# Moving the output projection of two head groups into the filler beside the sparse mixer, and grouping value products by four blocks, in a hybrid decoder layer

## The chip, the cores and the metric

One core of one Trainium2 chip runs the whole kernel. The metric is the time of one execution on the device in microseconds (us). Times below are medians of several runs; the profile is that of one execution.

## What is computed

One layer of a decoder trunk over 1024 tokens of width 1024, in float32. Four groups of four heads (head width 64) are projected from one normalised input, each with its own attention: A differential, B forgetting, C stick-breaking, D native sparse with a compressed, a selected and a windowed branch. With 1024 tokens the selection of 16 blocks of 64 takes every block, so the selected branch is a causal attention over all keys.

```python
h = rmsnorm(x, norm_mix_g) * (1 + sc_a) + sh_a
proj = h @ w_in                                  # columns of A, B, C and D
o_a = diff_attention(...);  o_b = forgetting_attention(...)
o_c = stick_breaking_attention(...);  o_d = native_sparse_attention(...)
mixed = concatenate([o_a, o_b, o_c, o_d], -1) @ w_out
x = x + gt_a * mixed
h = rmsnorm(x, norm_ffn_g) * (1 + sc_m) + sh_m
x = x + gt_m * conv_ffn(h, w_up, conv_w, conv_b, w_down)
```

## The kernel before

The kernel is a list of operations with a planner in front of it. Each call (K.mm, K.copy, K.dma and so on) records an operation with the tiles that it reads and writes; all of them are issued from one helper, which is why every row of the profile names line 392. At the end K.schedule() plays the list through: each engine takes, of the operations that are ready, the one that was recorded first. The order of recording is thus the priority, and it also gives out the buffers: a class of tiles (line 538 and after: name, quota, group, phase) hands out its tiles strictly in the order of recording, and a class of a later phase gets only what the earlier ones of its group can't claim. PSUM has 8 banks; while the mixers run, 4 are of class S (scores), 2 of class T (all transposes), 1 of class O (values) and 1 of class pP (projections).

What is recorded in which order is written by generators. merge(main, side, per) steps through a mixer and lets a filler follow: each step of the mixer yields its weight (1.3 for each 128 keys of a step of 128 queries), times a rate from RATES, and the filler is stepped until its own yields have used that up. The mixers come in the order A, C, D, B, with the rates 0.8, 0.6, 0.3 and 1.6. Beside A, C and D the filler is side(): the input projections still missing (cq, ck, dk, dq, vb, bq, bk, each of 8 token tiles and 24 products a tile, with a normalisation and transposes after every second tile) and the compression of keys. What is left of it after D is run to its end. Then out_AC() becomes the filler of B: it loads and splits the blocks 0, 1, 4 and 5 of w_out (scaled by gt_a, split into a high and a low part), and for each of 8 token tiles loads the outputs of A and C, transposes them (class T), splits them (oT) and forms 2 x 12 products of 128x512 in pP, which VectorE adds to x (x1p) for writing to x1. The other half of the projection, for D and B, follows after B and normalises its result for the feed-forward network.

The weights of the mixers' steps: A, B and C yield 46.8 for each of two head pairs, D 85.8. A projection's token tile yields 2.56, as does half a token tile of out_AC().

pv_pair() multiplies a step's probabilities with the values. Probabilities of two 128-key blocks and two heads are transposed into one T bank, copied to a pt tile, and for each block one planned operation (mm2) does two products, whose outputs are the two halves of the partitions of O:

```python
for j in range(g0, g1):
    c = 2 * (j - g0) * 128
    K.mm2([dst[0:64], dst[64:128]], vfn(j), [pt[:, c:c + 128], pt[:, c + 128:c + 256]], j == 0, j == nb - 1)
```

Of the kernel before, what the change touches and what calls it, by code (L numbers as in the profile page):

```python
# [13 lines left out]
OP = mybir.AluOpType  # L14
# [9 lines left out]
LAM_INIT = 0.8 - 0.6 * math.exp(0.0)  # L24
TOEP = 383
CL = 126
RATES = (0.8, 0.6, 0.3, 1.6)
STEP = 1.3
EARLY = 2
DCUT = (2, 3, 3, 3)  # L30

CA_Q, CA_K, CA_V = 0, 256, 512
CB_Q, CB_K, CB_V, CB_F = 768, 1024, 1280, 1536
# [110 lines left out]
class Program:  # L144
# [274 lines left out]
    def mm2(self, outs, lhsTs, rhss, start, stop):  # L419
# [6 lines left out]
        d = max(d, 1.26 * self._mm_use(lhsTs[0], rhss[0]))  # L426
        self.op([("PE", d, f)], list(lhsTs) + list(rhss), list(outs)).share = 2.0 * self._mm_use(lhsTs[0], rhss[0]) / d

    def tr(self, out, in_, ident):
        self.op([("PE", 109.0, self._call("tensor", "transpose", (out, in_, ident), {}))], [in_, ident], [out])  # L430

# [69 lines left out]
def layer_kernel(ctx: ExitStack, tc, x, c, rel_bias, ada_w, ada_b, norm_mix_g, norm_ffn_g, w_in, w_out,  # L501
# [4 lines left out]
    K = Program(tc)  # L506
    NB, NH = 33, 28
    pool = lambda n, b, **k: ctx.enter_context(tc.tile_pool(name=n, bufs=b, **k))
    cp, bp, hp, sp = pool("cp", 1), pool("bp", 1), pool("hp", 1), pool("sp", 1)
# [7 lines left out]
    def const(shape, dt=F32, name="const"):  # L517
        ncls[0] += 1
        k = f"c{ncls[0]}_{name}"
        K.klass(k, 1, "c", 0)  # L520
        return K.tile(k, shape, dt, name)

    def dram(shape, name):
        ncls[0] += 1
        k = f"d{ncls[0]}_{name}"
        K.klass(k, 1, "d", 0)
        return K.tile(k, shape, F32, name)
# [6 lines left out]
    for name, quota, group, phase in (  # L534

# [7 lines left out]

# [6 lines left out]

# [2 lines left out]
        K.klass(name, quota, group, phase)  # L553

    def blk(cls, dt=F32, shape=(128, 1024)):
        return K.tile(cls, shape, dt)

    def hb(cls, dt=F32):
        return K.tile(cls, (128, 512), dt)

    def ps1(cls):
        return K.tile(cls, (128, 512))


    ident = const([128, 128], name="ident")
# [55 lines left out]
    def halves(h):  # L621
        return slice(h * 512, h * 512 + 512)
# [42 lines left out]
    def row_tile(cls, src):  # L665
        t = blk(cls)
        K.dma(t, src.strided(0, [[0, 128], [1, D]]), 524288)
        return t
# [76 lines left out]
    def split_w(hcls, raw, shape):  # L745
        hi, lo = blk(hcls, F32R, shape), blk(hcls, F32R, shape)
        K.copy(hi, raw, ("ACT",))
        K.tt(lo, raw, hi, OP.subtract, ("POOL",))
        return hi, lo
# [70 lines left out]
    def qk_proj(name, col, scale, norm=None, early=False):  # L820
        return proj([(col, 256)], 256, qk_post([split_out((name, p), scale) for p in range(2)], norm and (norm, 0)), early=early)
# [68 lines left out]
    def pv_pair(P, n, vfn, dst):  # L890

        nb = n // 128
        for g0 in range(0, nb, 2):
            g1 = min(nb, g0 + 2)
            t = ps1("T")
            for j in range(g0, g1):
                for u in range(2):
                    c = 2 * (j - g0) + u
                    K.tr(t[:, c * 128:(c + 1) * 128], P[u][:, j * 128:(j + 1) * 128], ident)
            pt = hb("pt")  # L900
            w = (g1 - g0) * 256
            K.copy(pt[:, :w], t[:, :w])
            for j in range(g0, g1):
                c = 2 * (j - g0) * 128
                K.mm2([dst[0:64], dst[64:128]], vfn(j), [pt[:, c:c + 128], pt[:, c + 128:c + 256]], j == 0, j == nb - 1)

    def back(o):

# [121 lines left out]
    def compress():  # L1030
        kv = blk("kv")
        kvs.append(kv)

        def keep(jj, ps):
            K.copy(kv[:, jj * 256:jj * 256 + 256], ps)
        yield from proj([(CD_KC, 128), (CD_KS, 64), (CD_KW, 64)], 256,
                        qk_post([keep, split_out(("dk", 0), g_sw)], (64, 128)))
# [229 lines left out]
    def merge(main, side, per):  # L1267

        acc = 0.0
        for t in main:  # L1270
            acc += per * t
            while acc > 0.0:
                d = next(side, None)
                if d is None:
                    break
                acc -= d

    def chain(*gs):
        for g in gs:
            yield from g  # L1280

    def run_all(g):
        for _ in g:
            pass

    def heads(stacks, attn):
        for p in range(2):
            yield from attn(p, stacks(p))
# [68 lines left out]
    gta_row, gtm_row, ada_m = dram([1, D], "gta_row"), dram([1, D], "gtm_row"), {}  # L1357
# [15 lines left out]
    done = set()  # L1373

    def side():

        gs = [("cq", qk_proj("cq", CC_Q, 0.125)), ("ck", qk_proj("ck", CC_K, 1.0)), ("dk", compress()),
              ("dq", qk_proj("dq", CD_Q, g_dq, 64)), ("cmp", compress_kv()), ("vb", proj([(CB_V, 256)], 256, post_vb)),
              ("bq", qk_proj("bq", CB_Q, g_bq, 64)), ("bk", qk_proj("bk", CB_K, g_bk, 64))]
        next(gs[0][1])  # L1380
        for a, (name, g) in enumerate(gs):
            if a + 1 < len(gs):
                next(gs[a + 1][1])
            yield from g
            done.add(name)

    fill = side()
    for need, g, rate in (("", heads(stacks_A, attn_A), RATES[0]), ("ck", heads(stacks_C, attn_C), RATES[1]),
                          ("cmp", heads(stacks_D, attn_D), RATES[2])):
        while need and need not in done:  # L1390
            next(fill)
        merge(g, fill, rate)
    run_all(fill)


    gt_a = row_tile("gta", gta_row)
    wo_hi, wo_lo = {}, {}

    def load_wo(ks):
        for k in ks:  # L1400
            raw = blk("wor")
            K.dma(raw, w_out[0, k * 128:(k + 1) * 128, :], 524288)
            K.tt(raw, raw, gt_a, OP.mult, ("POOL",))
            wo_hi[k], wo_lo[k] = split_w("wo", raw, (128, 1024))

    def o_part(i, c0, c1, pcls):
# [14 lines left out]
    def o_mul(ps, hl, ks, n):  # L1421
        m = 0
        for t, k in enumerate(ks):
            for a, b in ((hl[0], wo_hi), (hl[1], wo_hi), (hl[0], wo_lo)):
                K.mm(ps, a[:, t, :], b[k][:, halves(n)], m == 0, m == 11)
                m += 1

    x1 = {}

    def out_AC():  # L1430
        load_wo((0, 1, 4, 5))
        yield 0
        for i in range(NT):
            hl = o_part(i, (0, 2), (4, 6), "T")
            x1[i] = dram([128, 1024], f"d_x1_{i}")
            for n in range(2):
                ps = ps1("pP")
                o_mul(ps, hl, (0, 1, 4, 5), n)
                xt = hb("x1p")
                K.dma(xt, x[0, i * 128:(i + 1) * 128, halves(n)], 262144)  # L1440
                K.tt(xt, ps, xt, OP.add)
                K.dma(x1[i][:, halves(n)], xt, 262144)
                yield 2.56
        load_wo((6, 7, 2, 3))
    oac = out_AC()
    next(oac)
    merge(heads(stacks_B, attn_B), oac, RATES[3])
    run_all(oac)

# [152 lines left out]
    chain, kept_b = {}, {}  # L1602
# [55 lines left out]
    def down_mul(n, ps=None):  # L1658
# [3 lines left out]
        q0 = 0  # L1662
        for c in DCUT:
            ops = {}
# [58 lines left out]
    done = K.schedule()  # L1723
# [29 lines left out]
```

## Time and profile before

| | us |
|---|---|
| median of 3 runs | 1491.72 |
| all three | 1491.72, 1485.66, 1492.05 |
| the profiled execution | 1490.82 |
| its span, first to last instruction | 1489.1 |

The mean granted clock of TensorE over the profiled span is 0.978 of full speed. In the profile PE is TensorE's products, PEld its loads of the stationary operand, DVE is VectorE, ACT ScalarE, POOL GpSimd and SP the queue of most DMAs. The stages follow each other by their tiles: A until about 376 us, C until 514, D until 677, B until 786, then the second half of the output projection with the normalisation, and from about 875 us the feed-forward network.

### The profile page before, as it was taken

Reading aid. Unit: us, or ns where it says so; the run is one execution under the profiler, and the core shown is the slowest. Engines: PE = TensorE matmul, PEld = TensorE weight load, DVE = VectorE, ACT = ScalarE, POOL = GpSimd, SP = SyncE. Lnnn points to the kernel's source line nnn. Section 1 sums busy time; section 2 is a strip of 40 time slices with the busy share of each in tenths; the row PEclk is TensorE's granted clock in tenths of the full one; section 3 lists DMA queues with packets and bytes.
Section 4 is the critical chain, followed back from the end, with each engine's and each line's share of the span. In section 5 each row is a group of like instructions: output and inputs, shape, how many; then the busy total and the mean of one; then the engine's idle time right before and its main releaser. Section 6 shows DMA issues by size and latency. Waiting matters only on the chain.

```text
span 1489.1 us, 24140 instructions
## 1 busy us (share of the span) xinstructions
PE 1389.8 (93%) x8573; PEld 1174.1 (79%) x8573; DVE 1120.2 (75%) x2382; ACT 703.0 (47%) x1529; POOL 217.3 (15%) x249
## 2 busy tenths in 40 slices
PE   3999999999799998999999789999999999999998
PEld 2878888888687886777877568888888888888886
DVE  7966668999779986775475886666666665898777
ACT  2531245657678655663364644334444443453342
POOL 3543310223323355100000000000000000000000
PEclk9999999999899998999999899999999999999999
DMA  9679463535431423145534322222222224963675
GB/s 353 209 213 319 134 171 93 170 91 155 114 76 49 133 92 98 41 105 162 161 105 155 113 86 86 80 83 85 85 85 80 84 85 169 370 238 99 226 248 170
DMA packets 169963, 211.24 MB, mean 142 GB/s; under 512 B 25517, under 2 KB 112214, under 8 KB 169842
## 3 DMA queue, kind: packets, MB, share of 16 engines
q1 hardware_dynamic: 168338, 208.52, 44.9%
q0 software_dynamic: 1504, 1.17, 0.5%
q8 instruction: 67, 1.10, 0.3%
q14 instruction: 54, 0.44, 0.1%
HBM read 165.30 MB, written 47.89 MB: 143 GB/s over the span
## 4 chain that ended last, share of the span: by engine, by line
PE 71%; DVE 12%; ACT 2%; issue 1%; DMA 1%; POOL 0%; SPq 0%; DVEq 0%; POOLq 0%; ACTq 0%
PE up L392 28%; PE dn L392 14%; PE pP L392 10%; PE T L392 7%; PE O L392 5%; PE S L392 4%; DVE P L392 4%; PE op L392 3%; ACT P L392 1%; DVE S L392 1%; DVE m L392 1%; DVE pt L392 1%; DVE nt L392 1%; DVE gB L392 1%; DVE hl L392 1%
## 5 line engine op out<-in xcount | busy, mean ns | idle before, releaser
L392 PE MATMUL up<-gB,fw 128*128 128x512 f32 x1320 | 303.6, 389 | 5.7 <-DVE fw L392 2.9
L392 PEld LDWEIGHTS up<-gB,fw 128*128 128x128 f32 x1320 | 247.5, 188 | 58.2 <-DVE fw L392 3.3
L392 PE MATMUL dn<-ds 128*128 128x512 f32 x924 | 209.9, 389 | 0.2 <-DVE ds L392 0.2
L392 PEld LDWEIGHTS dn<-ds 128*128 128x128 f32 x924 | 173.4, 188 | 36.6 <-DVE ds L392 0.6
L392 PE MATMUL pP<-wh,hT 128*128 128x256 f32 x1344 | 198.3, 292 | 3.4 <-DVE nt L392 1.3
L392 PEld LDWEIGHTS pP<-wh,hT 128*128 128x128 f32 x1344 | 178.7, 195 | 9.3 <-DVE nt L392 2.1
L392 ACT ACTIVATE P<-S,nm 128x512 f32<-128x512 f32 (+3 forms) x240 | 135.4, 571 | 81.9 <-DVE nm L392 63.6
L392 PE MATMUL S<-kst,qst 128*128 128x512 f32 (+2 forms) x480 | 134.0, 372 | 9.7 <-ACT P L392 5.7
L392 PE MATMUL up<-gA,fw 128*128 128x512 f32 x528 | 126.8, 395 | 7.6 <-DVE fw L392 7.6
L392 PE MATMUL T<-ident,P 128*128 128x128 f32 x696 | 113.1, 285 | 14.9 <-ACT P L392 8.9
L392 PEld LDWEIGHTS up<-gA,fw 128*128 128x128 f32 x528 | 99.8, 190 | 29.2 <-DVE fw L392 8.6
L392 PEld LDWEIGHTS T<-ident,P 128*128 128x128 f32 x696 | 79.8, 144 | 33.6 <-issue 15.1
L392 PEld LDWEIGHTS S<-kst,qst 128*128 128x128 f32 x480 | 79.1, 193 | 22.8 <-ACT P L392 9.0
L392 ACT COPY pt<-T 128x512 f32<-128x512 f32 (+1 forms) x106 | 56.5, 539 | 67.3 <-PE T L392 66.2
L392 DVE COPY pt<-T 128x512 f32<-128x512 f32 (+1 forms) x94 | 58.5, 627 | 38.6 <-PE T L392 36.1
L392 DVE TENSOR_REDUCE m<-S 128x1 f32<-128x512 f32 (+3 forms) x160 | 76.6, 488 | 7.5 <-PE S L392 6.7
L392 ACT CAST ds<-dg 128x512 fp32r<-128x512 f32 x82 | 48.2, 619 | 63.7 <-DVE dg L392 40.3
L392 DVE TENSOR_TENSOR fw<-fr,fw 128x512 fp32r<-128x512 f32 x110 | 75.1, 684 | 0.0
L392 ACT CAST fw<-fr 128x512 fp32r<-128x512 f32 x110 | 67.5, 614 | 9.6 <-DVE fw L392 9.5
L392 ACT ACTIVATE P<-P 128x256 f32<-128x256 f32 (+8 forms) x98 | 64.9, 690 | 11.5 <-POOL P L392 7.5
L392 PE MATMUL O<-pt,V 128*64 128x128 f32 x864 | 65.7, 287 | 4.2 <-DVE pt L392 2.3
L392 DVE SCALAR_TENSOR_TENSOR acc<-ada,cact,acc 128x512 f32<-128x512 f32 (+1 forms) x70 | 66.5, 950 | 3.1 <-DMA ada<-in_ada_w_dram 1.9
(295 smaller groups left out, 2323.2 us busy)
## 6 DMA issues: line engine op xcount, KB each, us to landing
dg<-d_g SPq DMA_DIRECT2D x99, 256.0 KB
fr<-in_ffn_w_up_dram SPq DMA_DIRECT2D x88, 256.0 KB
ada<-in_ada_w_dram SPq DMA_DIRECT2D x64, 256.0 KB
dg<-in_ffn_w_down_dram SPq DMA_DIRECT2D x55, 256.0 KB
d_g<-va SPq DMA_DIRECT2D x22, 512.0 KB
ada<-in_ada_w_dram SPq DMA_DIRECT2D x16, 512.0 KB
wr<-in_w_in_dram SPq DMA_DIRECT2D x32, 256.0 KB
x<-in_x_dram SPq DMA_DIRECT2D x8, 512.0 KB
```

Of the source, the lines that this page charges most:

```text
L392: return getattr(getattr(self.nc, eng), meth)(*a, **k)
```

## The change

The rate beside D goes from 0.3 to 0.45. out_AC() is no longer the filler of B alone: it is chained behind side(), so that one filler runs through all four mixers, and what follows the projection bk in it is the loading of the output weights and the projection of A and C. The row gt_a is loaded inside out_AC() and no longer between D and B. B stays at 1.6 for whatever filler is left. In pv_pair() the products of up to four blocks (PVB) are recorded as one operation, mms, behind the transposes and copies of all of them, and class pt has 4 tiles instead of 3. The planner costs such a group at 190 ns and 1.03 times the time of its pairs.

```diff
-RATES = (0.8, 0.6, 0.3, 1.6)
+RATES = (0.8, 0.6, 0.45, 1.6)
+PVB = 4
...
+    def mms(self, prods):
+        fs = [self._call("tensor", "matmul", (o, a, b), dict(start=st, stop=sp)) for o, a, b, st, sp in prods]
+        def f():
+            return [g() for g in fs][-1]
+        d = len(prods) * 0.5 * 1.03 * self._mm_use(prods[0][1], prods[0][2]) + 190.0
+        u = len(prods) * self._mm_use(prods[0][1], prods[0][2])
+        self.op([("PE", d, f)], [x for p in prods for x in p[1:3]], [p[0] for p in prods]).share = u / d
...
-            ... ("pt", 3, "h", 2), ...
+            ... ("pt", 4, "h", 2), ...
...
-        for g0 in range(0, nb, 2):
-            g1 = min(nb, g0 + 2)
-            t = ps1("T")
...
-                K.mm2([dst[0:64], dst[64:128]], vfn(j), [pt[:, c:c + 128], pt[:, c + 128:c + 256]], j == 0, j == nb - 1)
+        for h0 in range(0, nb, PVB):
+            h1 = min(nb, h0 + PVB)
+            pts = []
+            for g0 in range(h0, h1, 2):
+                g1 = min(h1, g0 + 2)
+                t = ps1("T")
...
+                pts += [pt[:, c:c + 128] for c in range(0, w, 128)]
+            K.mms([(dst[64 * u:64 * u + 64], vfn(j)[u], pts[2 * (j - h0) + u], j == 0, j == nb - 1)
+                   for j in range(h0, h1) for u in range(2)])
...
-    fill = side()
-    for need, g, rate in (("", heads(stacks_A, attn_A), RATES[0]), ("ck", heads(stacks_C, attn_C), RATES[1]),
-                          ("cmp", heads(stacks_D, attn_D), RATES[2])):
-        while need and need not in done:
-            next(fill)
-        merge(g, fill, rate)
-    run_all(fill)
-    gt_a = row_tile("gta", gta_row)
...
     def out_AC():
+        gt_a.append(row_tile("gta", gta_row))
         load_wo((0, 1, 4, 5))
         yield 0
...
-    oac = out_AC()
-    next(oac)
-    merge(heads(stacks_B, attn_B), oac, RATES[3])
-    run_all(oac)
+    fill = chain(side(), out_AC())
+    for need, g, rate in (("", heads(stacks_A, attn_A), RATES[0]), ("ck", heads(stacks_C, attn_C), RATES[1]),
+                          ("cmp", heads(stacks_D, attn_D), RATES[2]), ("", heads(stacks_B, attn_B), RATES[3])):
+        while need and need not in done:
+            next(fill)
+        merge(g, fill, rate)
+    run_all(fill)
```

## Rows read from the trace of the kernel before

**Rows 1.** The page: the span, the busy time of the engines (us, share of the span, instructions), and one line of the span in 40 equal slices (busy tenths of TensorE).
```profile
span 1489.1 us, 24140 instructions
...
PE 1389.8 (93%) x8573; PEld 1174.1 (79%) x8573; DVE 1120.2 (75%) x2382; ACT 703.0 (47%) x1529; POOL 217.3 (15%) x249
...
PE   3999999999799998999999789999999999999998
```

**Rows 2.** The table of stages: a stretch in us from the span's start, its length, then busy us and (instructions) of PE, PEld, DVE, ACT and POOL, then the granted clock of TensorE, the DMA engines' busy share and GB/s.
```profile
514.00:534.00 20.00, 18.73 (x161) 16.20 (x160) 17.30 (x48) 10.29 (x28) 9.60 (x6) 1.00 0.54 172
534.00:573.00 39.00, 39.00 (x358) 33.00 (x357) 27.88 (x70) 21.85 (x55) 24.32 (x26) 1.00 0.28 82
573.00:591.00 18.00, 11.18 (x59) 8.60 (x59) 17.17 (x61) 10.22 (x32) 8.05 (x5) 0.73 0.12 41
591.00:634.00 43.00, 39.58 (x340) 32.26 (x337) 30.71 (x101) 25.93 (x77) 9.37 (x5) 0.95 0.25 65
634.00:677.00 43.00, 39.62 (x368) 32.54 (x367) 31.75 (x119) 25.54 (x75) 2.93 (x3) 0.96 0.36 91
677.00:743.00 66.00, 66.00 (x392) 52.42 (x392) 30.65 (x66) 19.05 (x50) 0.68 (x1) 1.00 0.56 178
743.00:786.00 43.00, 42.00 (x381) 33.25 (x377) 31.09 (x91) 23.94 (x67) 0.00 (x0) 1.00 0.33 97
```

**Rows 3.** The same view in slices of 20 us, in the second half of the sparse mixer; the columns are those of Rows 2.
```profile
590.00:610.00 20.00, 18.02 (x165) 14.88 (x161) 12.91 (x47) 11.04 (x31) 7.82 (x4) 0.96 0.53 140
610.00:630.00 20.00, 18.56 (x154) 14.80 (x152) 14.71 (x51) 13.26 (x40) 1.59 (x2) 0.91 0.05 14
630.00:650.00 20.00, 17.20 (x145) 14.39 (x144) 14.05 (x44) 10.47 (x27) 1.04 (x1) 0.91 0.35 93
```

**Rows 4.** The tiles of the output projection: instructions with count, duration in ns (smallest/median/largest), first and last start in us, form.
```profile
L392 PE MATMUL T<-ident,oin x32: 270/272/332, 675.8 to 733.9; 128*128 128x128 f32 x32
...
L392 ACT CAST oT<-T x8: 585/586/586, 676.5 to 734.2; 128x512 fp32r<-128x512 f32 x8
L392 DVE TENSOR_TENSOR oT<-T,oT x8: 680/680/692, 677.5 to 735.0; 128x512 fp32r<-128x512 f32 x8
...
L392 DVE TENSOR_TENSOR x1p<-pP,x1p x16: 691/692/693, 681.3 to 742.4; 128x512 f32<-128x512 f32 x16
```

**Rows 5.** The timeline, two instructions: a start in us, its duration in us, engine, line, operation. The write of C's last results, and the end of the split of the fourth of eight blocks of output weights.
```profile
515.46 0.45 SPq L392 DMA_DIRECT2D o_dram<-on  x1
...
545.45 2.36 POOL L392 TENSOR_TENSOR wo<-wor,wo 128x1024 fp32r<-128x1024 f32 x1 [3.26 <-ACT wo L392]
```

**Rows 6.** The timeline of TensorE: a run of twelve products of the output projection and what follows it.
```profile
682.29 2.89 PE L392 MATMUL pP<-wo,oT 128*128 128x512 f32 x12
685.11 0.66 PE L392 MATMUL O<-pt,V 128*64 128x128 f32 x8
```

**Rows 7.** The timeline of TensorE: runs of value products (128x64, written to O) and the instruction after each; 214.88 is the first and 782.07 the last of 74 runs on V, 523.51 the first and 672.30 the last of 46 runs on VD.
```profile
214.88 0.44 PE L392 MATMUL O<-pt,V 128*64 128x128 f32 x4 [0.42 <-DVE pt L392]
...
523.51 0.44 PE L392 MATMUL O<-pt,VD 128*64 128x128 f32 x4
...
534.80 0.44 PE L392 MATMUL O<-pt,VD 128*64 128x128 f32 x4
535.17 0.66 PE L392 MATMUL T<-ident,P 128*128 128x128 f32 x4
...
557.43 1.09 PE L392 MATMUL T<-ident,P 128*128 128x128 f32 x8
558.28 0.94 PE L392 MATMUL S<-kst,qst 128*128 128x512 f32 x3
...
559.15 1.09 PE L392 MATMUL O<-pt,VD 128*64 128x128 f32 x16
560.18 0.66 PE L392 MATMUL T<-ident,P 128*128 128x128 f32 x4
...
672.30 1.31 PE L392 MATMUL O<-pt,VD 128*64 128x128 f32 x20
...
782.07 1.09 PE L392 MATMUL O<-pt,V 128*64 128x128 f32 x16
```

**Rows 8.** The timeline of VectorE: the results of B that are scaled for writing, first head pair's second half, then the second pair's first.
```profile
754.63 0.68 DVE L392 TENSOR_TENSOR on<-T,rlb 128x512 f32<-128x512 f32 x1
...
763.30 0.68 DVE L392 TENSOR_TENSOR on<-T,rlb 128x512 f32<-128x512 f32 x1
```

**Rows 9.** The page's groups for the copies of transposed probabilities (busy us, mean ns of one | idle before), and from the tile view of O the idle time ahead of value products by what ended it (us, times).
```profile
L392 ACT COPY pt<-T 128x512 f32<-128x512 f32 (+1 forms) x106 | 56.5, 539 | 67.3 <-PE T L392 66.2
L392 DVE COPY pt<-T 128x512 f32<-128x512 f32 (+1 forms) x94 | 58.5, 627 | 38.6 <-PE T L392 36.1
...
  ACT pt L392: 8.8, 19
...
  DVE pt L392: 6.8, 17
```

**Rows 10.** The timeline around the end of the filler: the last products of bk, the last step of their normalisation on VectorE, and the transposes that end the wait (in brackets the engine's idle time before and what ended it).
```profile
572.58 0.62 PE L392 MATMUL pP<-wh,hT 128*128 128x256 f32 x3
...
583.53 2.70 DVE L392 TENSOR_TENSOR nt<-nt,qk_y 128x256 f32<-128x256 f32 x2
585.95 1.24 PE L392 MATMUL T<-ident,nt 128*128 128x128 f32 x4 [3.53 <-DVE nt L392]
```

More of the change, by code (lines that the diff above doesn't have):

```diff
@@ L892, in pv_pair @@
         nb = n // 128
-        for g0 in range(0, nb, 2):
-            g1 = min(nb, g0 + 2)
-            t = ps1("T")
[L896 to L904, printed above, removed]
-                K.mm2([dst[0:64], dst[64:128]], vfn(j), [pt[:, c:c + 128], pt[:, c + 128:c + 256]], j == 0, j == nb - 1)
+        for h0 in range(0, nb, PVB):
[4 more added lines that the diff above has]
+                t = ps1("T")
+                for j in range(g0, g1):
+                    for u in range(2):
+                        c = 2 * (j - g0) + u
+                        K.tr(t[:, c * 128:(c + 1) * 128], P[u][:, j * 128:(j + 1) * 128], ident)
+                pt = hb("pt")
+                w = (g1 - g0) * 256
+                K.copy(pt[:, :w], t[:, :w])
+                pts += [pt[:, c:c + 128] for c in range(0, w, 128)]
+            K.mms([(dst[64 * u:64 * u + 64], vfn(j)[u], pts[2 * (j - h0) + u], j == 0, j == nb - 1)
+                   for j in range(h0, h1) for u in range(2)])
     def back(o):
@@ L1385, in side @@
             done.add(name)
-    fill = side()
-    for need, g, rate in (("", heads(stacks_A, attn_A), RATES[0]), ("ck", heads(stacks_C, attn_C), RATES[1]),
-                          ("cmp", heads(stacks_D, attn_D), RATES[2])):
-        while need and need not in done:
-            next(fill)
-        merge(g, fill, rate)
-    run_all(fill)
-    gt_a = row_tile("gta", gta_row)
-    wo_hi, wo_lo = {}, {}
+    wo_hi, wo_lo, gt_a = {}, {}, []
     def load_wo(ks):
@@ L1402, in load_wo @@
             K.dma(raw, w_out[0, k * 128:(k + 1) * 128, :], 524288)
-            K.tt(raw, raw, gt_a, OP.mult, ("POOL",))
+            K.tt(raw, raw, gt_a[0], OP.mult, ("POOL",))
             wo_hi[k], wo_lo[k] = split_w("wo", raw, (128, 1024))
```

2 rows, old and new, of the table k are left out of this document.

## The prediction

> **What bounds the kernel now.** I read the page's shares first, then the table of stages, then 20 us slices of the lossy one, then single instructions. TensorE is busy for 93% of the span; VectorE for 75%, ScalarE 47%, and no other engine comes near [rows 1]. A busy TensorE gains nothing from a new order, so the question is only where it is idle or runs at the lower of its two clock levels (1.2 instead of 2.4 GHz). The feed-forward network, from 875 us on, is solid. Before it the table of stages shows a pattern [rows 2]. While the sparse mixer D has filler beside it, TensorE works 39.00 of 39 us (534 to 573). Then the filler ends: 11.18 of 18 us at a mean clock of 0.73, and after that 39.58 and 39.62 of 43 us at 0.95 and 0.96. From 677 on the output projection of A and C lies beside B: 66.00 of 66 us at 1.00. B's rest, 743 to 786, has no filler either, yet loses only 1.00 of 43 us. So the change moves filler from B, which hardly needs it, to the part of D that does.
>
> **Where the moved work can start.** The projection's transposes take banks of class T, and each class hands out its tiles in the order of the program text. Before, these tiles stood behind all of D's, so the first one runs at 675.8 us [rows 4], although the four blocks of weights that it needs were split at 545.45 + 2.36 = 547.8 us, and C's last results went out at 515.46 [rows 5]; neither weights nor data are an obstacle. The loading of the weights itself (GpSimd, ScalarE, SP queue) ran beside D already; buffers set its pace, and its place in the order gains nothing. Now the tiles stand inside D. Filler is dealt out by credits: side() holds 150.9 of them, A and C draw 0.8 x 93.6 + 0.6 x 93.6 = 131, and D's own steps sum to 171.6. At 0.3 the remaining 19.9 last for 66 of D's 171.6 units (the filler's end at 573 us); at 0.45 they last for 44, and the projection's 16 x 2.56 = 41 go until unit 135. That covers the stretch that lost most and leaves D's last 36 units and all of B without.
>
> **Part 1, D's lossy stretch is filled.** Loss by slices of 20 us, from 590 to 650 [rows 3]: idle 1.98 + 1.44 + 2.80 = 6.2 us. Time at the lower level is twice (1 - clock) x 20: 1.6 + 3.6 + 3.6 = 8.8 us; TensorE was busy in 53.8 of the 60 us and does half the work at that level, so 8.8 x 0.90 / 2 = 4.0 us. Together 10.2 us. A filled stretch isn't free of loss: 514 to 573 left 1.27 us of 59 idle [rows 2], so some 118 us (this stretch and the moved work) lose 2.5, and 7.7 are left; as D's last 36 units stay bare, I take **-7 us**; bounds -10.2 (filled as 534 to 573) and -1 (the idle time stays, rival 1).
>
> **Part 2, B opens without filler.** The moved work is 16 x 12 products and 32 transposes. A run of 12 products begins at 682.29 and the next instruction at 685.11 us [rows 6], so 0.235 us each and 45 in all; eight transposes take 557.43 to 558.28 us [rows 7], 0.11 each, 3 in all. In the 66 us from 677 on B therefore got 18 us of work done, and this is the part that now has no cover. At the loss of 743 to 786 (1.00 of 43) it costs 0.4 us; at that of D's 610 to 650, idle 4.2 and slow 3.2 of 40 us [rows 3], 3.3 us. The first is the nearer: same mixer, and it holds the change from one head pair to the next (results at 754.63 and 763.30 [rows 8]). I take **+1.5**. B's end isn't bare: the last projection starts to fill in as soon as the first token tiles of the second pair are out.
>
> **Part 3, value products in fours.** Where a run of value products (128x64) starts and where the next instruction starts gives its price: 1 block 534.80 to 535.17, 0.37 us, 4 blocks 559.15 to 560.18, 1.03 us [rows 7] (four records of the trace are one block). That is 0.22 a block and 0.15 a run. The text had 196 groups of two blocks and now has 120 of four (24 for each of A, B, C, 48 for D). But in the trace the twos already stand together: 120 runs, 74 on V and 46 on VD [rows 7] (the first and the last of each stand there). What can still join are the 24 groups whose remainder is one or two blocks: its copy ends during the 1.03 us of the full four. 24 x 0.15 = 3.6, of which TensorE gains what it is bound for, some nine tenths: **-3**, bounds 0 and -7. The other side is that eight products now wait for the later of two copies (0.54 on ScalarE, 0.63 on VectorE [rows 9]). Idle ahead of value products on a copy was 8.8 + 6.8 = 15.6 us for 120 runs [rows 9], 0.13 each; if it doubles where no filler is (some 36 groups) that is +4.7. Behind a waiting group stand, in TensorE's order, the next transposes and scores, and for them both copying engines; the list of ready work can put them first, so **+1**, bounds 0 and 4.7. The fourth pt buffer takes a place that has no other taker in D and B; nothing. In A and C the order changes by part 3 alone.
>
> A row for a rule: the 0.15 us a run is what a change between 128x128 and 128x64 tiles costs here. The Trainium skill, TensorEngine Tiling (Array Packing), section Key Properties, says that a change of tiling mode drains the engine; the trace agrees. Taken by itself, from groups as the text has them, it would give 76 changes fewer, 76 x 0.15 = 11 us; the count of runs above says that they were already gone.
>
> **Part 4, the stall at the filler's end.** bk's last products end at 573.2 us; their normalisation goes through a chain of VectorE, ScalarE and GpSimd steps that ends from 583.53 on, and their transposes come at 585.95, after 3.53 us of idle TensorE, with all of D's later T tiles behind them [rows 10]. The 18 us lose 6.82 idle and 9.7 slow x 0.62 / 2 = 3.0 [rows 2]. The same last step exists after the change, earlier in D, and what follows it needs a T bank as well. I leave it at **0**: bounds -7 (denser filler brings the last step before D needs its turn) and +4 (the next T tiles wait for two DMAs of o_dram that can only be issued then). DMAs of the moved step, 2 + 4 for each token tile, pass the SP queue in D, where the DMA engines are used 0.25 to 0.36 [rows 2]; POOL issues nothing new. VectorE gets 0.68 + 2 x 0.69 = 2.1 us for each of 8 tiles [rows 4], against 62.5 of 86 us used from 591 to 677 [rows 2]: it has room.
>
> **Sum.** -7 + 1.5 - 3 + 1 + 0 = -7.5 us. The profiled execution took 1490.82 us (span 1489.1 and 1.7 around it), so **1483 us**. It lies 0.9 us under the median of the three runs, 1491.72, whose lowest is 1485.66; against the median it is -0.6%. About 0.5% (7.5 us, so a bound at 1484.3) is what a measurement of this kernel can tell from no change.
>
> **Rivals.** (1) The gain does not come: D's idle time is not a lack of work but the order of T tiles, as at 585.95, and the moved work queues in the same order. Part 1 is then -1, the time 1489. For it: in the stall of [rows 10] no filler could go ahead. Against: 534 to 573, 39.00 of 39 us in the same mixer with filler.
> (2) B alone is as lossy as D's 610 to 650: part 2 is 3.3 and, as D's bare end loses likewise, part 1 is 1 less: the sum -4.7, 1486. Against it 743 to 786.
> (3) Slower: a T bank as the bound. Each token tile holds one of the two T banks from its transpose (675.8) over ScalarE's cast (676.5) to the end of VectorE's subtraction (677.5 + 0.7) [rows 4], 2.4 us, in a stage whose every block needs those banks. If D's transposes stand still for all of it, 8 x 2.4 = 19 us come on top: 1502. It decides from 1.9 us a tile on, (7.5 + 7.5) / 8. Against: B shared the banks in the same way and TensorE was busy 66.00 of 66 us; but D's VectorE is fuller.
> (4) The stall of part 4 is covered: -7 more, 1476.
> (5) The fours join as strongly as the twos did, 196 to 120: then 120 become 73, -7 instead of -3: 1479. The rule of the Trainium skill's page above carries no further than this.
>
> **How the numbers follow.** Forecast (1478 to 1488) 0.40, rival 1 0.20, rival 2 0.10, rival 3 0.10, rival 4 0.12, rival 5 0.08. Two thirds of the forecast's own spread lie under 1484.3, so faster is 0.26 + 0.12 + 0.08 = 0.46; slower (above 1499) is rival 3 with a little of the bounds' far ends, 0.11; same 0.43. The range takes in rivals 1, 2, 4 and 5 with some of their spread and leaves rival 3 out: 1473 to 1496.
>
> **What would show it.** Transposes from oin beginning near 560 us and not at 676; the projection's products spread over some 100 us of D; TensorE near 100% at clock 1.00 there; D ending near 720 us; B from there to 779 at 95% or more; runs of value products below 105 in number; a T tile that waits 10 us or more near 555 to 570 (part 4). Wrong would be: idle slices in D beside unfinished projection work (rivals 1 and 3), clock under 0.95 in B (rival 2), or a feed-forward stage that takes another length than before, which nothing here touches.

## The result, and the profile after

The changed kernel takes 1472.57 us (median of 4, 1470.88 to 1473.88) against 1491.88 us before (median of 4): ratio 0.9885, 95% interval 0.9861 to 0.9909. It is faster, as forecast, but by 1.15% and not by 0.6%, and it lies 0.4 us under the low end of the range. The profiled execution took 1470.88 us.

The page's first lines of the changed kernel (span; busy us, share and instructions of each engine), which answer to [rows 1]:

```profile
span 1469.2 us, 24142 instructions
...
PE 1379.6 (94%) x8573; PEld 1171.3 (80%) x8573; DVE 1118.4 (76%) x2384; ACT 701.1 (48%) x1524; POOL 226.7 (15%) x252
```

The span is 19.9 us shorter, the busy time of TensorE 10.2 us. The table of stages, with the columns of [rows 2], until the filler's end, the stall, D beside the projection, D's end, B:

```profile
513.00:550.00 37.00, 35.49 (x314) 32.11 (x314) 28.89 (x79) 21.41 (x56) 26.13 (x21) 1.00 0.48 148
550.00:565.00 15.00, 11.73 (x101) 9.90 (x100) 13.79 (x32) 6.96 (x21) 9.09 (x13) 0.94 0.18 42
565.00:673.00 108.00, 107.76 (x784) 88.72 (x783) 66.83 (x204) 50.35 (x135) 16.87 (x8) 0.99 0.42 135
673.00:706.00 33.00, 31.41 (x301) 25.83 (x301) 28.61 (x112) 21.46 (x66) 2.55 (x2) 1.00 0.41 95
706.00:765.00 59.00, 58.09 (x531) 47.32 (x528) 42.39 (x125) 37.20 (x107) 0.00 (x0) 1.00 0.35 96
```

D is now full where it was lossy: beside the projection TensorE works 107.76 of 108 us. The stall at bk's end is 15 us with 11.73 busy, where it was 18 with 11.18. B, now without the projection of A and C beside it, loses 0.91 of 59 us. The projection's transposes run in D, from 558.3 and not from 675.8 us [rows 4]:

```profile
L393 PE MATMUL T<-ident,oin x32: 270/273/332, 558.3 to 664.0; 128*128 128x128 f32 x32
```

Value products, TensorE's timeline: the first and the last run on VD, a long run and what follows it, the last run on V. Over the whole trace there are 98 runs, 63 on V and 35 on VD. Counted in the same way the kernel before has 119; [rows 7] and the prediction have 120, because one run on VD that lay across the edge of two windows of the timeline was counted twice:

```profile
520.42 0.44 PE L393 MATMUL O<-pt,VD 128*64 128x128 f32 x4
...
577.20 1.97 PE L393 MATMUL O<-pt,VD 128*64 128x128 f32 x32
579.10 0.66 PE L393 MATMUL T<-ident,oin 128*128 128x128 f32 x4
...
699.76 1.31 PE L393 MATMUL O<-pt,VD 128*64 128x128 f32 x20
...
760.93 1.09 PE L393 MATMUL O<-pt,V 128*64 128x128 f32 x16
```

Eight blocks in one run take 1.90 us (577.20 to 579.10), which is 8 x 0.22 and one 0.15, as in [rows 7].

**Where the time went.** C's last result is issued for writing at 515.46 us before [rows 5] and at 512.80 now, B's last at 785.73 and 764.57. So the 19.9 us are 2.7 before D, 18.5 in D and B (270.3 to 251.8 us), and -1.2 behind B. For the same stretch I add up, in slices of 10 us, the idle time of TensorE and half of its busy time at the lower clock level: 15.9 + 6.2 = 22.1 us before, 7.5 + 1.7 = 9.2 now. The rest of the stretch, 248.2 and 242.6 us, is work at full clock. So 12.9 us are lost time that is gone and 5.6 us are less work. The forecast had 5.5 for the first (parts 1, 2, 4) and 2 for the second (part 3).

### The profile page after: what moved, and what is told of

It reads as the page before. It is cut to its first block, busy times and chain, and to the rows that moved or that the text cites. A ratio compares the mean times of both kernels' runs of the same rounds, so it can differ in the third digit from the quotient of the medians.

```text
span 1469.2 us, 24142 instructions
## 1 busy us (share of the span) xinstructions
PE 1379.6 (94%) x8573; PEld 1171.3 (80%) x8573; DVE 1118.4 (76%) x2384; ACT 701.1 (48%) x1524; POOL 226.7 (15%) x252
## 4 chain that ended last, share of the span: by engine, by line
PE 71%; DVE 13%; issue 2%; ACT 2%; POOL 1%; DMA 0%; POOLq 0%; DVEq 0%; ACTq 0%
PE up L393 28%; PE dn L393 14%; PE pP L393 10%; PE T L393 7%; DVE P L393 4%; PE S L393 4%; PE O L393 4%; PE op L393 3%; DVE pt L393 1%; DVE m L393 1%; DVE S L393 1%; ACT P L393 1%; DVE gB L393 1%; DVE nt L393 1%; DVE hl L393 0%
## 5 line engine op out<-in xcount | busy, mean ns | idle before, releaser
L393 ACT ACTIVATE P<-P 128x128 f32<-128x128 f32 (+8 forms) x98 | 64.0, 690 | 20.1 <-POOL P L393 16.3
L393 DVE SCALAR_TENSOR_TENSOR cv<-ga,ccol,cv 128x1023 f32<-128x1023 f32 (+1 forms) x44 | 56.5, 1283 | 15.8 <-ACT cv L393 15.0
```

What stands on the lines that cost most here:

```text
L393: return getattr(getattr(self.nc, eng), meth)(*a, **k)
```

## The experiments

The table has all runs. Loss and work are those of D and B, worked out as above from each run's profiled execution; the ratio is against the kernel before in the same rounds. Held is explained in part 3: in the same stretch, what VectorE's instructions beside GpSimd's operations on output weights took beyond their usual time (the median of their kind beside no instruction of GpSimd), counted where it is over 0.2 us.

| kernel | us | ratio, 95% | runs of value products | D and B, us | loss | work | held, us |
|---|---|---|---|---|---|---|---|
| before | 1491.88 | | 119 | 270.3 | 22.1 | 248.2 | 8.6 |
| changed | 1472.57 | 0.9885 (0.9861 to 0.9909) | 98 | 251.8 | 9.2 | 242.6 | 6.7 |
| fours alone | 1478.41 | 0.9928 (0.9909 to 0.9946) | 99 | 259.5 | 16.7 | 242.8 | 6.1 |
| move alone | 1493.66 | 1.0031 (1.0011 to 1.0051) | 121 | 270.7 | 21.0 | 249.7 | 16.5 |
| changed, pairs in mms | 1476.02 | 0.9924 (0.9898 to 0.9950) | 116 | 255.0 | 7.8 | 247.2 | 4.2 |
| changed, rate 0.3 | 1485.44 | 0.9972 (0.9955 to 0.9989) | 98 | 266.2 | 22.3 | 243.9 | 3.8 |
| before, pairs in mms | 1489.85 | 1.0000 (0.9982 to 1.0019) | 115 | 262.7 | 16.4 | 246.3 | 10.3 |
| changed, old price | 1475.35 | 0.9904 (0.9871 to 0.9937) | 97 | 247.2 | 5.2 | 242.0 | 4.3 |
| changed, weights on VectorE | 1471.74 | 0.9867 (0.9833 to 0.9900) | 99 | 253.1 | 9.0 | 244.1 | 0 |
| move alone, weights on VectorE | 1478.66 | 0.9913 (0.9886 to 0.9939) | 120 | 255.2 | 7.2 | 248.0 | 0 |
| before, weights on VectorE | 1481.49 | 0.9939 (0.9920 to 0.9959) | 117 | 262.5 | 15.0 | 247.5 | 0 |
| fours alone, weights on VectorE | 1475.63 | 0.9901 (0.9881 to 0.9920) | 100 | 255.7 | 11.1 | 244.6 | 0 |
| changed, price 150 | 1476.20 | 0.9902 (0.9881 to 0.9924) | 97 | 256.8 | 13.6 | 243.2 | 11.1 |
| before, price 1.30 | 1487.49 | 0.9987 (0.9970 to 1.0003) | 116 | 261.9 | 15.1 | 246.8 | 6.3 |

D and B are not the whole difference. C's last write goes out between 510.9 and 524.4 us, and latest in three kernels whose planner has another price for value products: 520.0 in changed with pairs in mms, 518.1 in before with pairs in mms, 524.4 with the old price. What these save in D and B they partly lose in A and C, and a profiled execution can lie some us off its kernel's median.

**1. The parts one by one.** Fours alone is the kernel before with the new pv_pair, mms and the fourth pt tile; move alone is the changed kernel with the old pv_pair:

```diff
 # fours alone, against the kernel before
-            K.mm2([dst[0:64], dst[64:128]], vfn(j), ...)
+            K.mms([... for j in range(h0, h1) for u in range(2)])
-  ("pt", 3, "h", 2)
+  ("pt", 4, "h", 2)
 # move alone, against the changed kernel: the same lines turned round
```

> The kernel before with the value products in fours (mms, PVB 4, four pt tiles) and nothing else: filler, rates and place of the output projection as before. Theory M (the move carries the gain: TensorE's idle time and low clock in D vanish, the fours only save some 20 runs of 0.15 us): 3 to 6 us faster than before, about 1487, the losses between 573 and 650 us stay. Theory K (the fours carry it, by fewer runs and by a planner whose price for a run is nearer to the chip): 10 us or more, 1481 or less.

> The changed kernel with value products in twos as before (mm2, three pt tiles): only the filler is chained and the rate beside D is 0.45. Theory M: 13 to 15 us faster than before, 1477 to 1479, with about 120 runs of value products and D nearly without idle time beside the projection. Theory K: at most the forecast's 7 us, 1484 or more.

Both expectations of theory M fell, and both times lie in theory K's ranges. The fours alone gave 0.72%, the move alone nothing: it is 0.1 to 0.5% slower. In the fours alone two stretches of stages, the 18 us behind bk's end and D's bare stretch, read:

```profile
562.00:580.00 18.00, 17.71 (x183) 15.03 (x181) 16.79 (x64) 13.05 (x39) 8.17 (x11) 1.00 0.41 108
580.00:665.00 85.00, 76.77 (x669) 64.42 (x666) 63.39 (x219) 52.61 (x153) 17.63 (x10) 0.92 0.28 77
```

The loss of the bare stretch is still there (76.77 of 85 us, clock 0.92), but the stall is not: 17.71 of 18 us, where [rows 2] had 11.18 at a clock of 0.73. Nothing in the fours makes a stall of bk's normalisation shorter. And in the move alone D beside the projection isn't full; its rows for that stretch and for B:

```profile
569.00:690.00 121.00, 113.10 (x789) 90.75 (x790) 73.22 (x211) 49.53 (x135) 17.25 (x8) 0.97 0.38 120
723.00:784.00 61.00, 59.36 (x529) 45.74 (x530) 42.40 (x128) 38.66 (x108) 0.00 (x0) 1.00 0.35 93
```

7.90 of 121 us are idle there, at a clock of 0.97, although the same products as in the changed kernel are its filler. So the filler was in the right place and something else held TensorE up.

**2. Price and rate.** The planner charges the new groups otherwise than the old ones, and it settles the order. Pairs in mms is the changed kernel, and in a second run the kernel before, with the new operation for two blocks; old price charges the fours 269 ns a block; and the rate alone was put back:

```diff
-PVB = 4
+PVB = 2
 # the changed kernel; the same with the projection beside B
...
-        d = len(prods) * 0.5 * 1.03 * self._mm_use(...) + 190.0
+        d = len(prods) * 0.5 * max(self._mm_time(...), 1.26 * self._mm_use(...))
...
-RATES = (0.8, 0.6, 0.45, 1.6)
+RATES = (0.8, 0.6, 0.3, 1.6)
```

> The changed kernel with PVB 2: the new operation and its price (190 ns a run) stay, the groups are of two blocks again. If the fours matter by what is joined, the runs rise towards 120 and the time by 3 us or so, to 1475 to 1477, like the move alone. If they matter by the planner's truer price, the time stays at 1471 to 1474.

> The kernel before with the new operation and its price of 190 ns a run, but groups of two blocks (PVB 2), four pt tiles, the output projection beside B as before. Theory R (the planner's price of a run makes the better order): about as fast as the fours alone, 1476 to 1481. Theory J (what is joined counts): 118 to 120 runs and the time of before, 1487 to 1491. Theory N (every order of the planner is a draw, since it does not know which small VectorE operations will stand behind a GpSimd operation): anything from 1476 to 1493.

> The changed kernel with its groups of four, but the planner charges them as it charged the twos, 269 ns a block and nothing for the run. Theory R: the gain of the price goes, 1482 or more. Theory J: 100 runs or so and 1471 to 1475. Theory N: between, and the loss sits where small VectorE operations run beside GpSimd.

> The changed kernel with the old rate 0.3 beside D: the projection of A and C still follows side() in the filler, but begins at unit 66 of D's 171.6 and some 9 of its 41 credits are left for B. If the gain is that D's bare stretch is filled, nearly all of it stays, 1473 to 1478, with the stall at bk's end back near 573 us at its old size of about 10 us. If the rate matters by itself, 1480 or more.

The price isn't it (theory R): pairs at the new price gain nothing beside B (1.0000), and fours at the old price keep nearly all, 0.9904 and 97 runs. These two, and the changed kernel with pairs, came within 0.4 us of theory J's ranges, but the move alone is no 1475 to 1477. What the column of work shows is the grouping: seven kernels with pairs need 246.3 to 249.7 us, 247.7 on average, seven with fours 242.0 to 244.6, 243.3 on average. That is 4.4 us, in every order. The loss has no such rule: 5.2 to 22.3 us. The move alone and changed with pairs, both with groups of two and the projection in D, lie at 21.0 and 7.8, and 17.6 us apart in time. They differ in the price, in two blocks being one operation, and in the fourth pt tile; no run tells these three apart. That fits theory N, whose range nearly any time would have fitted.

The old rate was a miss: I expected 1473 to 1478, it is 1485. Its stretch beside the projection, the change from D to B, and TensorE's first scores of B:

```profile
571.00:704.00 133.00, 123.74 (x915) 100.58 (x915) 82.24 (x265) 61.45 (x177) 17.46 (x10) 0.96 0.40 121
704.00:725.00 21.00, 19.95 (x120) 15.61 (x119) 12.30 (x33) 7.73 (x22) 0.00 (x0) 0.84 0.19 64
...
703.74 1.29 PE L393 MATMUL S<-kst,qst 128*128 128x512 f32 x4 [3.38 <-DMA qst<-d_bq]
```

Spread over 150 us the projection no longer fills D (9.26 of 133 us idle, clock 0.96), and at the start of B the scores wait 3.38 us for their DMA, which nothing covers. So the rate belongs to the gain, as far as one order can show it.

**3. Who holds TensorE up.** In the move alone, 588 us, one line each for GpSimd, VectorE (two), ScalarE and TensorE:

```profile
588.00 2.36 POOL L393 TENSOR_TENSOR wor<-wor,gta 128x1024 f32<-128x1024 f32 x1 [3.73 <-DMA wor<-in_w_out_dram]
...
588.11 2.27 DVE L393 TENSOR_TENSOR dl<-dl 128x8 f32<-128x8 f32 x1
590.30 0.35 DVE L393 CUSTOM_DVE_ANT_0 S<-S,bias,nm 128x128 f32<-128x128 f32 x1
...
590.74 0.69 ACT L393 ACTIVATE P<-S,nm 128x512 f32<-128x512 f32 x1 [3.23 <-DVE nm L393]
...
591.92 0.55 PE L393 MATMUL T<-ident,oin 128*128 128x128 f32 x3 [1.40 <-ACT P L393]
```

GpSimd scales a block of output weights, 2.36 us from 588.00. VectorE begins an addition of 8 columns at 588.11 and needs 2.27 us for it: it ends when GpSimd does. The minima queued behind it come 2 us late, ScalarE's exponentials after 3.23 us of waiting, and TensorE, whose order is fixed, stands 1.40 us in front of a transpose of the filler's own (oin), with the filler's products behind it. The stall of [rows 10] has the same in it. Two operations of VectorE there, one free and one beside GpSimd, and GpSimd's two:

```profile
580.72 0.16 DVE L392 TENSOR_TENSOR qk_t<-qk_t,qk_y 128x8 f32<-128x8 f32 x1
581.34 2.00 DVE L392 TENSOR_TENSOR qk_y<-qk_y,qk_t 128x8 f32<-128x8 f32 x1
...
580.97 2.35 POOL L392 TENSOR_TENSOR wo<-wor,wo 128x1024 fp32r<-128x1024 f32 x1 [3.52 <-ACT wo L392]
583.28 2.34 POOL L392 TENSOR_TENSOR wor<-wor,gta 128x1024 f32<-128x1024 f32 x1
```

An operation of 8 columns takes 0.16 us, the next 2.00; the scaling in [rows 10] that starts at 583.53 takes 2.70 beside the second GpSimd operation and, in a kernel without these, 0.76. In the changed kernel one such wait is left in the stall, 3.30 us:

```profile
546.61 3.03 PE L393 MATMUL pP<-wh,hT 128*128 128x256 f32 x24
...
557.68 3.30 DVE L393 TENSOR_TENSOR qk_t<-ss,qk_y 128x8 f32<-128x8 f32 x1
561.01 0.17 DVE L393 TENSOR_TENSOR qk_t<-qk_t,qk_y 128x8 f32<-128x8 f32 x1
...
558.59 2.35 POOL L393 TENSOR_TENSOR wo<-wor,wo 128x1024 fp32r<-128x1024 f32 x1
...
562.19 0.30 PE L393 MATMUL T<-ident,nt 128*128 128x128 f32 x1 [3.27 <-DVE nt L393]
```

The Trainium skill, SBUF — State Buffer, section Who interferes with whom, says so: VectorE's second SBUF port pair is GpSimd's, and a VectorE instruction with two inputs in SBUF contends with a GpSimd instruction that reads there. The traces agree, and give the price: the small operation ends with GpSimd's, in these lines 1.8 to 3.1 us late. The planner knows nothing of it, so which small operation meets which block of weights is a draw.

The column held adds such waits up. In D and B of all 14 traces no VectorE instruction went more than 0.2 us over its usual time without an instruction of GpSimd beside it. The move alone has the most, 10 instructions and 16.5 us. Among the five kernels with the projection in D at rate 0.45 and the weights on GpSimd, the loss goes with it, but for the first two, which are nearly equal: 4.2, 4.3, 6.7, 11.1 and 16.5 us held, 7.8, 5.2, 9.2, 13.6 and 21.0 us lost. That is also what sets the move alone apart from changed with pairs, whose order avoids most of the waits with GpSimd's work in place. It isn't all of the loss: at the old rate 22.3 us are lost with 3.8 held.

To test it, all 16 operations on output weights go to VectorE, in all four combinations of the two parts:

```diff
-            K.tt(raw, raw, gt_a[0], OP.mult, ("POOL",))
-            wo_hi[k], wo_lo[k] = split_w("wo", raw, (128, 1024))
+            K.tt(raw, raw, gt_a[0], OP.mult, ("DVE",))
+            wo_hi[k], wo_lo[k] = blk("wo", F32R), blk("wo", F32R)
+            K.copy(wo_hi[k], raw, ("ACT",))
+            K.tt(wo_lo[k], raw, wo_hi[k], OP.subtract, ("DVE",))
```

> The move alone, value products in twos as before, with the scaling and the low part of the output weights on VectorE. Theory P: it is these waits that ate the gain of the move alone (1493.7): now 1478 to 1486, and the filled stretch of D has under 3 us of idle TensorE in place of 7.9. Rival (the twos as such keep D from being filled): 1490 or more.

> The changed kernel with the scaling and the low part of the output weights on VectorE instead of GpSimd: 16 operations of 128x1024, about 1.1 us each, 18 us more on VectorE and 38 less on GpSimd. Theory P (in D small VectorE operations stand behind GpSimd's weight operations, and the exponentials and TensorE behind them): 2 to 6 us faster than the changed kernel, 1466 to 1470, no operation of 8 columns over 0.3 us in D, the stall at bk's end shorter by 3 us. Rival: VectorE's extra work costs as much as it saves, 1472 to 1478.

> The kernel before with the scaling and the low part of the output weights on VectorE; nothing else. Theory P (waits of small VectorE operations behind GpSimd's weight operations cost time wherever a plan lets them meet): the stall at bk's end loses the 3.5 us that two such waits added to it, and D some more: 1480 to 1486. Rival Q (those waits hurt only where the filler is moved into D): 1488 to 1492, the extra 18 us of VectorE bring nothing.

> The fours alone with the weight operations on VectorE: with the run before and the earlier ones this fills a table of four (twos or fours, projection beside B or in D) without GpSimd in the way. If the gain of the fours alone (11.5 us) was their own, it is 11 us here as well, measured against the kernel before with the weights on VectorE. If it came from an order that happened to avoid those waits, it is 3 to 5 us here, 1476 to 1481, what 20 fewer runs of 0.15 us give.

The move alone falls from 1493.7 to 1478.7 us, the kernel before from 1489.4 in those rounds to 1481.5, the fours alone from 1478.4 to 1475.6, and the changed kernel stays (1472.6 and 1471.7). The first two lie in theory P's ranges; the changed kernel's 1471.7 lies between P's range and the rival's. The fours alone gain 0.38%, 6 us, over the kernel before with its weights on VectorE, and not their 11.5, so by these medians a part of them came from the order; 1475.6 is 0.4 us below the range expected for that. The planner's order changes with the edit as well, so these times alone don't prove the waits; but in the move alone the loss falls from 21.0 to 7.2 us as the 16.5 us held go. The stall is nearly gone in the kernel before without GpSimd's operations, while its bare stretch is as lossy as ever:

```profile
559.00:577.00 18.00, 16.63 (x160) 13.16 (x159) 15.21 (x52) 11.86 (x30) 6.51 (x10) 1.00 0.44 128
577.00:668.00 91.00, 82.85 (x727) 68.65 (x726) 70.11 (x244) 54.27 (x164) 5.76 (x5) 0.94 0.26 68
```

In the changed kernel the chain behind bk now has its normal durations, and TensorE waits 0.78 us in place of 3.27:

```profile
554.04 0.16 DVE L393 TENSOR_TENSOR qk_t<-ss,qk_y 128x8 f32<-128x8 f32 x1
556.26 0.16 DVE L393 TENSOR_TENSOR qk_y<-qk_y,qk_t 128x8 f32<-128x8 f32 x1
556.74 0.76 DVE L393 TENSOR_TENSOR nt<-nt,qk_y 128x256 f32<-128x256 f32 x2
...
557.31 0.30 PE L393 MATMUL T<-ident,nt 128*128 128x128 f32 x1 [0.78 <-DVE nt L393]
```

Yet the filled stretch isn't free of idle time. In the move alone with the weights on VectorE:

```profile
564.00:680.00 116.00, 112.03 (x812) 90.60 (x811) 75.20 (x214) 49.90 (x135) 5.14 (x6) 1.00 0.39 125
```

3.97 of 116 us, where I expected under 3. And in the changed kernel with the weights on VectorE:

```profile
557.00:675.00 118.00, 113.43 (x819) 92.89 (x819) 73.93 (x215) 52.36 (x143) 2.56 (x2) 0.99 0.37 117
```

4.57 of 118 us idle, with nothing held. So the changed kernel's 0.24 of 108 was a good draw of the order, and what it gains in the stall without GpSimd's operations it loses here.

**4. How much is a draw.** Two prices of the planner were moved a little; no instruction is added or left out:

```diff
 # the changed kernel
-        d = ... + 190.0
+        d = ... + 150.0
 # the kernel before, in mm2
-        d = max(d, 1.26 * self._mm_use(lhsTs[0], rhss[0]))
+        d = max(d, 1.30 * self._mm_use(lhsTs[0], rhss[0]))
```

> The changed kernel with the planner's price of a run at 150 ns in place of 190; no instruction is added or left out, only the order moves. It measures how much a time depends on the draw of an order. If little: 1471 to 1475. If the order is a draw with the GpSimd waits as its dice: up to 1483.

> The kernel before with its price for value products at 1.30 instead of 1.26, 9 ns more a block; no instruction is added or left out. If the order matters little: 1487 to 1492. If the kernel before was a bad draw: 1480 to 1486, and a stall at bk's end that is shorter than 10 us.

3.6 us more for the one, 1 us above what I expected if the order matters little; 1.9 less for the other, inside that range, though its stall is shorter (2.5 us of TensorE idle from bk's last product to the end of its transposes, for 6.7 in the kernel before). Neither interval is clear of the kernel it started from. So single differences of 2 to 4 us between these kernels prove nothing, and the 17.6 us of part 2 show that an order can be worth far more. What stands is the averages of seven and the waits that were read in the traces.

## Why it came out so

| | pairs | fours |
|---|---|---|
| projection beside B, weights on GpSimd | 1 | 0.9928 |
| projection in D, weights on GpSimd | 1.0031 | 0.9885 |
| projection beside B, weights on VectorE | 0.9939 | 0.9901 |
| projection in D, weights on VectorE | 0.9913 | 0.9867 |

Below, where GpSimd is out of the way, the parts add up: the move gives 0.26% and 0.34% (4 and 5 us), the fours 0.38% and 0.46% (6 and 7 us), both 0.72%, 10.7 us. Only the sum is well clear of the intervals; the two differences of the move are not. Above they don't add up: -0.31 and 0.43% for the move, 0.72 and 1.46% for the fours. The difference between above and below is what GpSimd's operations on the weights cost: 0.61% or 9 us in the kernel before, 0.18% or 3 us in the changed one. So of the 17 us some 11 are the change's own, and some 6 come because the new order happens to suffer less from GpSimd. That is luck, and how it comes about isn't shown: the time held itself only falls from 8.6 to 6.7 us. Each of these differences holds a draw of the order too, so the shares are rough. The 15 us that the move alone gets back go with 16.5 us held that are gone.

**Parts 1 and 2, -7 and +1.5: about right, with luck.** By the tables of stages, D behind the stall loses 10.4 us before and 2.9 after, B 1.0 before (677 to 786) and 0.9 after: -7.5 and 0. But the move alone did not bring that, and the filled stretch of the changed kernel was a good draw. Once nothing of GpSimd's disturbs it, the move by itself gives 4 to 5 us for a forecast of 5.5, within the noise of these runs. Where it starts (558 us for a forecast of 560), what it covers and how little B loses without it (0.91 of 59 us) came as forecast; D ended at 706 and not at 720 us because of the other parts.

**Part 3, -3 and +1: mis-sized.** The fours give 6 to 7 us. 21 runs fewer came, for 24 forecast, and a run costs 0.15 us. But the work in D and B falls by 4.4 us, while the 16 runs that D and B have fewer (70 to 54) account for 2.4. Summed up by tiles, from one product's start to the next at full clock, the value products give 2.2 us of the 4.4; 0.9 are products of the input projections, of which 4 to 5 more run before C's last write and so are no saving; most of the rest is in scores and transposes, and its cause is open. The +1 for waiting on the second copy doesn't show: idle time ahead of value products on a copy is 10.5 us (1.1 on ScalarE's, 9.4 on VectorE's), for 15.6 before [rows 9].

**Part 4, 0: the step that failed.** I read the stall's 9.8 us [rows 2, 10] as a matter of order at the filler's end and left it in place, with a bound of -7 and rival 4 at 0.12. In the changed kernel it loses 4.0 us (3.27 idle and 0.06 of 11.73), so the term is -5.8 and not 0. The chain behind bk is no shorter: from its last product to its transposes 12.8 us before (573.2 to 585.95) and 12.6 after (549.6 to 562.19). What changed is that TensorE had other work meanwhile, much as in the bound of -7 that I named and did not take. That, too, hangs on the order: in the fours alone and in changed with pairs TensorE doesn't idle there at all.

I also missed what is in the chain. I had looked at which operations it had, not at how long they took: 2.70 us for two operations of 256 columns stands in [rows 10]. Two waits behind GpSimd make up 3.8 us of it before, one makes up 3.1 in the changed kernel. In the same part I wrote that VectorE has room, from its busy share; a share counts the waits behind GpSimd as work. With the weights on VectorE, so without these waits, the kernel before is 8 to 9 us faster (6 to 12 by the interval; the planner's order changes with them too).

**The rivals.** Rival 1 is what happened to the move alone: idle time stayed in D beside work that stood ready. Its mechanism was not quite mine: TensorE stood in front of transposes until exponentials that were late had ended, 1.40 us at 591.92 in the lines above. Rivals 2 and 3 did not come: B lost little, and no T bank bound a stage whose TensorE was busy for 107.76 of 108 us. Rival 4 came for the most part, -5.8 of its -7 us. Rival 5's 73 runs did not come.

## What to carry to other kernels

Read the duration of small operations on a chain, not only their order and their engine's busy share: an operation of 8 columns that takes 2 us in place of 0.16 is waiting for something, here for GpSimd. When an order is fixed in advance, time each part alone and together before believing a sum, and take the disturbance that differs between the orders out of all four kernels. Count the disturbance in each trace as well, since taking it out changes the order. A filler is worth its place only if its rate fills the stretch and nothing in front of it in the queue waits.

## What the runs showed of the hardware

A VectorE addition of 8 columns with both inputs in SBUF took 0.16 us alone and 2.27 us beside a GpSimd operation of 128x1024 (2.36 us), ending with it. Another operation of 8 columns began at 557.68 us in the changed kernel, while GpSimd was still issuing DMAs, and ended at 560.98, when the operation that GpSimd began at 558.59 ended (560.94). The issue of DMAs alone doesn't hold such an operation: in the 14 traces 16 two-input operations of 8 columns began beside it and took their usual 0.15 to 0.17 us, and none of them had an operation on output weights beginning less than 2.35 us later. The three that were held (3.30, 4.21 and 4.44 us) had one beginning 0.91 to 2.05 us later, directly behind the DMAs. Why the wait starts that far ahead of the start that the trace gives for GpSimd is open. A run of value products of 128x64 costs 0.15 us besides 0.22 us a block, for one block as for eight.
